# Running log-sum-exp over 4 x 4096 x 4128: two-row tiles moved inside the batches, the engine order put off around them, and loads by rows for two tiles only

## Chip, cores and metric

The kernel runs on one core of a Trainium2 chip. The metric is the device time in microseconds of one execution; less is better. All data are float32, and the program is one launch.

## What is computed

For each of 4 batches and each of 4128 columns, a running log-sum-exp down 4096 rows:

```python
B, S, D = (4, 4096, 4128)
out[:, 0, :] = x[:, 0, :]
for t in range(1, S):
    mx = np.maximum(out[:, t - 1, :], x[:, t, :])
    out[:, t, :] = mx + np.log(np.exp(out[:, t - 1, :] - mx) + np.exp(x[:, t, :] - mx))
```

The input is normally distributed, so the kernel takes exp of it as it is, forms running sums, and takes the log. At the end it looks at the smallest first rows and the largest sums and branches to a slow general routine (`_general`) if they left a safe range; here they don't. The input is 270.5 MB and so is the output.

## The kernel before

**Tiles.** A tile is 128 x r consecutive rows of one batch, all 4128 columns, with r = 2 or 3: partition p holds rows r*p to r*p + r - 1 one behind the other, so a tile is one contiguous stretch of DRAM of r x 2064 KB. The lists `begin`, `usual` and `final` (lines 176 to 178) give r for the tiles of batch 0, of batches 1 and 2, and of batch 3: 12 + 11 + 11 + 12 = 46 tiles, ten with two rows ("short" tiles) and 36 with three, numbered 0 to 45 in the order in which they run. Four slots in SBUF hold four tiles; a tile is loaded, worked on in place, and stored from its slot.

**Work on a tile.** Its columns are cut into three chunks of 1376 (`Chunk`). For each chunk:

- `exp` on ACT (line 113), over all rows of the chunk.
- `sums` on DVE (lines 133 and 135): the sum over the partition's rows, into a buffer z for chunks 0 and 1, into the tile's last row for chunk 2.
- `head` on PE (line 142): a matmul with a triangular matrix, which gives each partition the sum of all rows above it into PSUM. For chunks 0 and 1 the running total of the tiles before comes in with z's last row. For chunk 2 `fold` (line 123) adds it to the first row on DVE, ahead of its `sums`.
- `add` on DVE (lines 157 and 165, or line 150 for chunk 2): the sum from above onto the rows.
- `log` on ACT (lines 173 and 174, or line 169 for chunk 2).

`least` (line 116) and `total` (line 126) run once per batch and chunk and serve the test of the range. There are two PSUM buffers, taken in turn.

**The order of the work is written out by hand.** Each engine has a list, built in the loop over tiles (lines 238 to 253), and runs it strictly in order, waiting for what each step needs. What varies by tile is the "turn": `turns.get(t, usual_turn)` gives two rows of four numbers. The first says how many chunks of tile t+1 have had their `exp` put on ACT's list before the `log` of tile t's chunk 0, chunk 1 and chunk 2, and after it. The second says the same of tile t+1's `sums` on DVE ahead of the `add` of tile t. The usual turn is `(0, 2, 3, 3), (0, 0, 1, 1)`: two `exp` of the next tile before the `log` of chunk 1, the third before that of chunk 2, and one `sums` of the next tile before the `add` of chunk 2. Six turns differ, at tiles 0 to 3, n-3 and n-2 (n = 46).

**Transfers.** All loads and stores are issued by SP, on one queue, in the order of the list `moves` (lines 193 to 202): loads 0 to 3, stores 0 and 1, then load 4, store 2, load 5, store 3 and so on; the last two loads follow each other. SP waits for what each needs (a store for its tile's last `log`, a load for the store that frees its slot) and issues nothing behind it until then. There are eight semaphores for transfers, taken in turn, so a transfer also waits until the one eight before it has landed. A tile's load is one transfer (line 93), but for tiles 0 to 6 (`BY_ROW = 7`) it is one transfer for each of its r rows (line 96).

Of the kernel before, what the change touches and what calls it, by code (L numbers as in the profile page):

```python
# [13 lines left out]
MM = 512  # L14
NC = 3
SLOTS = 4
BY_ROW = 7
PASSED = NC - 1
SMALL = 2.0 ** -63
LARGE = 2.0 ** 62  # L20
# [3 lines left out]
def kernel(  # L24
# [57 lines left out]
    class Step:  # L82
# [6 lines left out]
            return rows.rearrange("(p j) d -> p j d", j=self.r)  # L89

        def load(self):
            if self.n >= BY_ROW:
                nc.sync.dma_start(out=self.xt, in_=self.dram(x))
                return
            for j in range(self.r):
                nc.sync.dma_start(out=self.xt[:, j, :], in_=self.dram(x)[:, j, :])
# [76 lines left out]
            nc.scalar.activation(e, e, ACT.Ln)  # L173
            nc.scalar.activation(self.row[r - 1], self.z, ACT.Ln)  # L174

    begin = [2, 2, 3, 3, 3, 3, 3, 3, 3, 3, 2, 2]
    usual = [2, 3, 3, 3, 3, 3, 3, 3, 3, 3, 3]
    final = [2, 3, 3, 3, 3, 3, 3, 3, 3, 2, 2, 2]
    steps = []
    for b in range(B):  # L180
        row = 0
# [9 lines left out]
    n = len(steps)  # L191
# [3 lines left out]
    for t in range(n):  # L195
# [8 lines left out]
    lists = {"move": moves, "act": [], "vec": [], "pe": []}  # L204
    act, vec, pe = lists["act"], lists["vec"], lists["pe"]
    usual_turn = (0, 2, 3, 3), (0, 0, 1, 1)
    turns = {
# [4 lines left out]
        n - 3: ((0, 0, 3, 3), (0, 0, 0, 0)),  # L212
        n - 2: ((1, 2, 3, 3), (0, 0, 1, 1)),
    }
    given = {"exp": [0] * n, "sums": [0] * n}
# [158 lines left out]
```

## Time and profile before

| | us |
|---|---|
| median of 3 timed runs | 1266.24 (1265.36 to 1266.4) |
| the profiled execution, its own time | 1262.61 |
| its span, first to last instruction | 1260.6 |
| busy: DVE | 1047.2 (83%) |
| busy: ACT | 926.1 (73%) |
| busy: PE matmul | 601.3 (48%) |
| bytes moved over the span | 429 GB/s |

"Busy" is the time in which an engine had an instruction of the program under way. The profile gives the DMA engines' busy share beside it, and the chain of work that ended last, followed back from the end. Times in the views are counted from the first instruction. In the views of the profile, L12 is line 12 of the kernel, and SPq is SP's instruction queue.

### The profile page before, as it was taken

How to read it: one execution, taken by the hardware profiler on the slowest of the kernel's cores; microseconds unless marked ns; L12 is line 12 of the kernel's file. 1: busy time of each engine (PE TensorE's matmuls, PEld its weight loads, DVE VectorE, ACT ScalarE, POOL GpSimd, SP SyncE). 2: the span in 40 equal slices, each digit the busy share in tenths (PEclk: the TensorE clock that was granted, in tenths of full speed). 3: DMA queues.
4: the chain of work that ended last, by engine and by line, in shares of the span. 5: the costliest groups of instructions: out<-in, count | busy, mean ns of one | idle time of the engine just before them, and what ended most of it. 6: DMA issues, size and time to landing. Idle time of an engine off the chain costs nothing.

```text
span 1260.6 us, 3131 instructions
## 1 busy us (share of the span) xinstructions
PE 601.3 (48%) x830; PEld 233.9 (19%) x830; DVE 1047.2 (83%) x547; ACT 926.1 (73%) x369; POOL 3.8 (0%) x15
## 2 busy tenths in 40 slices
PE   3544444464545444445444544455454454445662
PEld 1221111121222111111111211121121121111220
DVE  4999888895899877888978978888897797888984
ACT  5968777776678677777857777777776677777882
POOL 1000000000000000000000000000000000000000
PEclk9866666676677676666765666666675666666676
DMA  9999999999999999999999999999999999999998
GB/s 398 426 441 427 428 435 434 424 434 431 438 434 429 425 443 434 429 428 436 429 442 428 439 432 428 433 442 429 429 435 426 434 412 442 430 429 433 430 423 375
DMA packets 14994, 541.28 MB, mean 429 GB/s; under 512 B 1664, under 2 KB 1664, under 8 KB 1664
## 3 DMA queue, kind: packets, MB, share of 16 engines
q1 hardware_dynamic: 14976, 541.07, 99.7%
q8 instruction: 7, 0.11, 0.0%
q14 instruction: 11, 0.09, 0.0%
HBM read 270.53 MB, written 270.53 MB: 429 GB/s over the span
## 4 chain that ended last, share of the span: by engine, by line
DMA 61%; ACT 22%; DVE 9%; issue 6%; SPq 1%; ACTq 0%; DVEq 0%
DMA x<-in_x_dram 57%; ACT x L113 11%; ACT x L169 5%; ACT x L173 4%; DMA out_dram<-x 4%; DVE x L150 2%; ACT x L174 2%; DVE x L157 2%; DVE z L135 1%; DVE x L133 1%; DVE z L160 1%; DVE x L135 0%; DVE x L123 0%; SPq L99 0%; DVE short L116 0%
## 5 line engine op out<-in xcount | busy, mean ns | idle before, releaser
L113 ACT ACTIVATE x<-x 128x4128 f32<-128x4128 f32 (+1 forms) x138 | 462.3, 3382 | 183.7 <-DMA x<-in_x_dram 183.6
L142 PE MATMUL p<-z,carried 128*128 128x512 f32 (+1 forms) x504 | 375.2, 910 | 456.4 <-DVE z L135 297.0
L173 ACT ACTIVATE x<-x 128x2752 f32<-128x2752 f32 (+1 forms) x92 | 206.0, 2239 | 129.7 <-DVE z L165 117.1
L133 DVE TENSOR_TENSOR x<-x 128x1376 f32<-128x1376 f32 x108 | 171.2, 1585 | 146.8 <-ACT x L113 146.8
L142 PEld LDWEIGHTS p<-z,carried 128*128 128x128 f32 x504 | 145.8, 309 | 687.4 <-DVE z L135 331.6
L142 PE MATMUL p<-x,summed 128*128 128x512 f32 (+1 forms) x276 | 194.3, 867 | 130.9 <-issue 125.1
L157 DVE TENSOR_TENSOR x<-p,x 128x2752 f32<-128x2752 f32 (+1 forms) x92 | 248.2, 2698 | 0.9 <-PE p L142 0.8
L150 DVE SCALAR_TENSOR_TENSOR x<-p,inner,x 128x4128 f32<-128x4128 f32 (+1 forms) x46 | 193.1, 4198 | 0.6 <-PE p L142 0.5
L135 DVE TENSOR_TENSOR z<-x 127x1376 f32<-127x1376 f32 x92 | 146.3, 1590 | 39.5 <-ACT x L113 33.7
L169 ACT ACTIVATE x<-x 128x4128 f32<-128x4128 f32 (+1 forms) x46 | 155.5, 3379 | 2.4 <-DVE x L150 2.4
L165 DVE TENSOR_TENSOR z<-x 128x1376 f32<-128x1376 f32 x84 | 133.8, 1592 | 2.9
L174 ACT ACTIVATE x<-z 128x1376 f32<-128x1376 f32 x92 | 122.7, 1333 | 0.0
L142 PEld LDWEIGHTS p<-x,summed 128*128 128x128 f32 x276 | 75.3, 290 | 248.5 <-issue 245.9
L135 DVE TENSOR_TENSOR x<-x 128x1376 f32<-128x1376 f32 x46 | 73.2, 1590 | 1.2
L123 DVE TENSOR_TENSOR x<-p,x 1x1376 f32<-1x1376 f32 x42 | 66.1, 1573 | 2.8 <-ACT x L113 2.4
L142 PE MATMUL p<-z,below 128*128 128x512 f32 (+1 forms) x48 | 31.9, 827 | 48.4 <-DVE z L135 28.7
L142 PEld LDWEIGHTS p<-z,below 128*128 128x128 f32 x48 | 12.7, 280 | 66.6 <-issue 31.0
L116 DVE TENSOR_REDUCE short<-x 1x1 f32<-1x1376 f32 x12 | 18.7, 1566 | 0.0
L160 DVE CUSTOM_DVE_ANT_0 z<-x 128x1376 f32<-128x1376 f32 x8 | 12.7, 1592 | 0.3
L126 DVE TENSOR_REDUCE probe<-p 1x1 f32<-1x1376 f32 x4 | 6.3, 1568 | 0.0
L308 PE MATMUL good<-ones,low 128*1 128x1 f32 x2 | 0.2, 164 | 5.5 <-DVE low L306 5.5
L74 POOL MEMSET z<- 128x1376 f32 x2 | 2.5, 1258 | 0.0
(21 smaller groups left out, 4.8 us busy)
## 6 DMA issues: line engine op xcount, KB each, us to landing
out_dram<-x SPq DMA_DIRECT2D x36, 6192.0 KB, 26.0
x<-in_x_dram SPq DMA_DIRECT2D x31, 6192.0 KB, 40.1
out_dram<-x SPq DMA_DIRECT2D x10, 4128.0 KB, 22.0
x<-in_x_dram SPq DMA_DIRECT2D x19, 2064.0 KB, 28.2
x<-in_x_dram SPq DMA_DIRECT2D x8, 4128.0 KB, 34.7
```

The costliest lines, as they stand in the source:

```text
L113: nc.scalar.activation(self.e, self.e, ACT.Exp)
L123: nc.vector.tensor_tensor(out=to, in0=pt[0:1], in1=to, op=ALU.add)
L133: nc.vector.tensor_tensor(out=e[1], in0=e[0], in1=e[1], op=ALU.add)
L135: nc.vector.tensor_tensor(out=self.z[0:n], in0=e[r - 2][0:n], in1=e[r - 1][0:n], op=ALU.add,)
L142: nc.tensor.matmul(self.pt[:, a:b], lhsT=w, rhs=self.z[:, a:b], start=True, stop=True,)
L150: nc.vector.scalar_tensor_tensor(out=self.e, in0=base, scalar=inner[:, 0:1], in1=self.e, op0=ALU.mult, op1=ALU.add,)
L157: nc.vector.tensor_tensor(out=e, in0=base, in1=e, op=ALU.add)
L160: nc.vector.tensor_tensor_reduce(out=self.z, in0=ends[0], in1=ends[1], scale=1.0, scalar=0.0, op0=ALU.add, op1=ALU.add, accum_out=probe[:, ...
L165: nc.vector.tensor_tensor(out=self.z, in0=ends[0], in1=ends[1], op=ALU.add)
L169: nc.scalar.activation(self.e, self.e, ACT.Ln)
L173: nc.scalar.activation(e, e, ACT.Ln)
L174: nc.scalar.activation(self.row[r - 1], self.z, ACT.Ln)
```

## The change

Three things are changed.

- The lists of rows per tile: the same number of two-row and three-row tiles in each batch, but the two-row tiles stand inside the batches instead of at their beginnings and ends, except for tiles 0 and 1 and the last two, which stay.
- The turns: a table of 21 entries in place of six. Around the short tiles many are `alone` in their second row (no `sums` of the next tile ahead of this one's `add`), with the `exp` of the next tile put later; some are `(0, 0, 0, 0)`, where nothing of tile t+1 runs on ACT or DVE until the `log` of tile t is on ACT's list. Turns 1 and 3 now put the third `exp` of the next tile ahead of the `log` of chunk 2, and one `sums` of it ahead of the `add` of chunk 2. The turn of n-3 becomes the usual one.
- Loads by rows for tiles 2 and 3 only, in place of tiles 0 to 6.

```diff
-BY_ROW = 7
+BY_ROW = (2, 3)
...
-            if self.n >= BY_ROW:
+            if self.n not in BY_ROW:
                 nc.sync.dma_start(out=self.xt, in_=self.dram(x))
...
-    begin = [2, 2, 3, 3, 3, 3, 3, 3, 3, 3, 2, 2]
-    usual = [2, 3, 3, 3, 3, 3, 3, 3, 3, 3, 3]
-    final = [2, 3, 3, 3, 3, 3, 3, 3, 3, 2, 2, 2]
+    begin = [2, 2, 3, 3, 3, 3, 2, 3, 2, 3, 3, 3]
+    usual = [3, 3, 3, 3, 3, 2, 3, 3, 3, 3, 3]
+    final = [3, 3, 3, 3, 2, 3, 2, 3, 3, 3, 2, 2]
...
     usual_turn = (0, 2, 3, 3), (0, 0, 1, 1)
+    alone = (0, 0, 0, 0)
     turns = {
         0: ((2, 3, 3, 3), (0, 0, 1, 1)),
-        1: ((1, 2, 2, 2), (0, 0, 0, 0)),
-        2: ((3, 3, 3, 3), (0, 0, 0, 0)),
-        3: ((2, 2, 3, 3), (0, 0, 0, 0)),
-        n - 3: ((0, 0, 3, 3), (0, 0, 0, 0)),
+        1: ((1, 2, 3, 3), (0, 0, 1, 1)),
+        2: ((3, 3, 3, 3), alone),
+        3: ((1, 2, 3, 3), (0, 0, 1, 1)),
+        6: ((0, 0, 0, 0), alone),
+        7: ((0, 0, 0, 0), alone),
+        9: ((0, 0, 1, 1), alone),
+        10: ((0, 2, 2, 2), alone),
+        11: ((0, 1, 2, 2), alone),
+        12: ((0, 2, 2, 2), alone),
+        13: ((0, 2, 2, 2), alone),
+        15: ((0, 1, 1, 1), alone),
+        17: ((0, 0, 3, 3), alone),
+        18: ((0, 0, 0, 0), alone),
+        26: ((0, 0, 1, 1), alone),
+        28: ((0, 0, 3, 3), alone),
+        29: ((0, 0, 0, 0), alone),
+        n - 10: ((0, 0, 1, 1), alone),
+        n - 8: ((0, 0, 1, 1), alone),
+        n - 6: ((0, 0, 3, 3), alone),
+        n - 5: ((0, 0, 3, 3), alone),
         n - 2: ((1, 2, 3, 3), (0, 0, 1, 1)),
     }
```

## The prediction

> **What bounds the kernel now.** I read the page first, for how full the DMA engines are.
>
> ```profile
> span 1260.6 us, 3131 instructions
> DMA  9999999999999999999999999999999999999998
> q1 hardware_dynamic: 14976, 541.07, 99.7%
> out_dram<-x SPq DMA_DIRECT2D x36, 6192.0 KB, 26.0
> x<-in_x_dram SPq DMA_DIRECT2D x31, 6192.0 KB, 40.1
> out_dram<-x SPq DMA_DIRECT2D x10, 4128.0 KB, 22.0
> x<-in_x_dram SPq DMA_DIRECT2D x19, 2064.0 KB, 28.2
> x<-in_x_dram SPq DMA_DIRECT2D x8, 4128.0 KB, 34.7
> ```
>
> One queue carries 541 MB, and its packets fill 99.7% of sixteen engines' span. The busy digit is 9 in 39 of the 40 slices. The last five rows are the transfers by kind: the last number of each is the time from issue to landing, so it holds the wait in the queue too. Whether the queue is ever empty is asked of a table of windows (us, busy time of PE, PEld, DVE, ACT and POOL, granted clock, DMA share, GB/s):
>
> ```profile
> 2.00:50.00 48.00, 20.71 (x36) 8.46 (x36) 34.02 (x21) 33.76 (x18) 2.36 (x6) 0.92 1.00 425
> 10.00:48.00 38.00, 20.71 (x36) 8.46 (x36) 32.02 (x20) 31.67 (x16) 0.00 (x0) 0.91 1.01 431
> 350.00:600.00 250.00, 121.70 (x162) 47.04 (x160) 213.98 (x106) 188.25 (x71) 0.00 (x0) 0.66 1.00 433
> 2.00:1246.00 1244.00, 601.34 (x830) 233.89 (x830) 1047.24 (x547) 924.94 (x369) 2.36 (x6) 0.67 1.00 431
> 1246.00:1261.00 15.00, 0.00 (x0) 0.00 (x0) 0.00 (x0) 0.00 (x0) 0.00 (x0) 0.50 0.71 303
> ```
>
> From 2 us to 1246 us the DMA share is 1.00. DVE is busy 1047 of those 1244 us and ACT 925, so neither fills the time. The kernel is a full transfer queue with under 2 us ahead of it and the last store's end behind it. So a change can win time only by moving the same bytes faster, and can lose time only where it lets the queue run dry.
>
> The second question is how close it comes to running dry. The chain of waits lists transfers from issue to landing (start, us, what):
>
> ```profile
> 38.21 24.71 DMA out_dram<-x
> ...
> 377.57 35.17 DMA x<-in_x_dram
> ...
> 548.06 40.14 DMA x<-in_x_dram
> 588.23 3.65 ACT x L113
> ...
> 689.45 35.26 DMA x<-in_x_dram
> ...
> 1003.25 36.19 DMA x<-in_x_dram
> ...
> 1195.51 20.07 DMA x<-in_x_dram
> ```
>
> At 433 GB/s a transfer of 6192 KB (6.34 MB) takes 14.6 us, one of 4128 KB 9.8, one of 2064 KB 4.9. The load issued at 548.06 landed 40.14 us later. It stood right behind a three-row store, so 40.1 - 2 x 14.6 = 10.9 us of work was still ahead of that store when it was issued. I call that the store's cover: what the queue holds when the store joins it, the start-up of the transfer included. The loads at 377.57, 689.45 and 1003.25 also follow three-row stores, and give 6.0, 6.1 and 7.0 us. Those are the thin places, and the share stays at 1.00 there too.
>
> **The cover, worked from the order.** SP issues store t, load t+3, store t+1, load t+4. Behind load t+1 the queue holds store t-1 and load t+2, and then store t. In a usual turn ACT runs two Exp of tile t+1 before the middle Ln of tile t, so store t follows the landing of load t+1 by a fixed lag:
>
> ```profile
> 606.12 0.34 SPq L99 DMA_DIRECT2D out_dram<-x  x1
> ...
> 1195.93 47.23 SPq L99 DMA_DIRECT2D out_dram<-x  x4
> ...
> 1214.82 0.34 SPq L99 DMA_DIRECT2D out_dram<-x  x1
> ...
> DMA to landing us min/median/max: 16.9/26.0/34.3
> L113 ACT ACTIVATE x<-x 128x4128 f32<-128x4128 f32 x108 | 388.8, 3632 | 155.2 <-DMA x<-in_x_dram 155.2
> L113 ACT ACTIVATE x<-x 128x2752 f32<-128x2752 f32 x30 | 73.5, 2485 | 28.5 <-DMA x<-in_x_dram 28.5
> ```
>
> The load landed at 588.2 (the Exp starts at 588.23) and the store was issued at 606.12: lag 17.9 us. The cover is store t-1 plus load t+2 less 17.9: 29.2 - 17.9 = 11.3 where both have three rows (10.9 was read off), and 24.4 - 17.9 = 6.5 where one of them has two (6.0 to 7.0 read off). So the rule holds to half a microsecond. If tile t+1 is the short one, its three Exp take 2485 instead of 3632 ns, and the lag is 14.5. The last store was issued at 1195.93 + 47.23 - 0.34 = 1242.8 and took 16.9 us to land, 9.8 of them its own: cover 7.1.
>
> **The change part by part.**
>
> *Loads by rows for tiles 2 and 3 only.* Nineteen loads of 2064 KB become six. In their place come three more loads of 6192 KB (34) and two more of 4128 KB (10). The bytes are the same, and there are 96 transfers for 104. The window of row loads alone ran at 431 GB/s, the window of whole-tile transfers at 433. Thirteen row loads fewer are 27.5 MB: 63.8 us at 431, 63.5 at 433, so -0.3 us. The rounding of both rows allows -0.1 to -0.5. If the row of 425, which holds the start, were the rate, it would be -1.2. I take -0.4, nearest to the cleaner pair of rows. No Exp waits differently for it, since each Exp reads all the rows of its tile.
>
> In the windows of row loads, ten transfers in 48 us left the share at 1.00, so no time between queued transfers shows. The Trainium skill's page "DMA: Bandwidth & Descriptors", in its section "Anatomy of one DMA — SWDGE (gpsimd) path", gives each DMA of another queue kind a fixed cost of about 2.0 us whatever its size. By that rule eight DMAs fewer would be an estimated 16 us; the trace does not bear it out for a full queue.
>
> *The two-row tiles moved inside the batches.* Both kernels have ten two-row and 36 three-row tiles, the same instructions and the same bytes. So nothing is removed on the path, and only the covers move. Before, the joints of the batches put a thin cover of 6 to 7 us at seven stores (8, 13, 21, 24, 32, 35, 41) and 7.1 at the last. After, by the same rule:
>
> - Store 1. Turn 1 now runs a third Exp of tile 2 ahead of the last Ln of tile 1, and DVE the first sums of tile 2 ahead of the last add.
>
> ```profile
> 50.37 2.48 ACT L169 ACTIVATE x<-x 128x2752 f32<-128x2752 f32 x1
> 38.21 15.01 SPq L99 DMA_DIRECT2D out_dram<-x  x2
> 46.31 3.08 DVE L150 SCALAR_TENSOR_TENSOR x<-p,inner,x 128x2752 f32<-128x2752 f32 x1
> ```
>
>   The Ln started at 50.37 and the store followed at 38.21 + 15.01 - 0.34 = 52.9. One Exp more is 3.6 us on ACT; on DVE the add is put off from 46.3 by two additions of 1.6, and ends inside that Exp. So the store is issued at 56.4. The store ahead of it lands at 38.21 + 24.71 = 62.9: cover 6.5 for 10.0.
> - Store 4. Load 6 is short: 14.6 + 9.8 - 17.9 = 6.5, for 11.3.
> - The last store. Tile n-3 has three rows for two. Its store follows the landing of load n-2 by 14.5 us, 9.8 of which load n-1 takes, so 4.7 after load n-1. From that store to the last one is 28.0 us, as before (1214.8 to 1242.8), so 32.7 in all. The queue holds 14.6 + 14.6 + 9.8 = 39.0: cover 6.3 for 7.1.
> - All other usual turns: 10 us or more, the thinnest with a short store ahead and a short tile next, 24.4 - 14.5 = 9.9.
>
> *The turns put off (no Exp of the next tile until the Ln of this one is done).* These make DVE and ACT wait for each other. Queued behind the waiting Exp are all later Exp, and SP's next store behind them. For a three-row tile alone, from its load's landing: one Exp 3.6, two sums of 3.1 each, the fold 1.6, the first add with its z 4.6, the third sum 3.1, the second add 4.6, the last add 4.4, the Ln 3.6: 31.7, about 33 with the hand-overs, for 29.2 of queue. The deepest is tile 7, after the put-off turns 6 and 7: behind its load stand stores 5 and 6 and loads 8 and 9, 14.6 + 9.8 + 9.8 + 14.6 = 48.8, so its store keeps 16 us. By the same sums the covers after the put-off turns 18 and 29 fall from 21 to 11. So these turns cost nothing while their cover is over zero. Should all cover be gone at a place, each us late costs one us, once, and the queue is full again after it.
>
> The order of the tiles, then, makes covers on the whole deeper (three thin ones for eight). Nothing was lost at the thin ones in this trace, so nothing is won there: 0, with a bound below, under the rivals.
>
> *Sum.* The profiled execution took 1262.6 us, 2.0 over its span; it is 3.6 us below the median of the timed runs, 1266.24 (1265.36 to 1266.4). -0.4 makes it 1262.2, and on the median **1265.8 us**.
>
> **The rivals.**
>
> *The timed runs run dry where the profiled one did not (faster).* What the 3.6 us between the profiled execution and the timed median are, the trace doesn't say. If they were all idle queue at the eight thin places, 0.45 each, and the change leaves three, 2.3 us go, with the 0.4 2.7: 1263.5. For it: a cover of 6 us has to hold the start-up of a transfer and whatever the sixteen engines have drifted apart. Against it: a share of 1.00 in every window.
>
> *Store 1 comes too late (slower).* Turn 1 puts an Exp and two additions ahead of a store whose cover was 10.0, and SP holds load 4 behind it. The cover I find is 6.5. Beyond it the queue stands empty: if turn 1 ran 9.5 us later than my sum, 3.0 would be lost, less 0.4: 1268.8. It would decide from an issue after about 62 us. Against it: each duration in the sum for turn 1 has its row, and one Exp is all that is added on ACT. The same price holds for store 4 and the last store.
>
> *The rate itself moves.* One GB/s on the mean of 431 is 2.9 us. The window of 425 GB/s at the start, and the 431 of the whole for 433 in the middle, show that it does move within a run. This widens the range on both sides and is no forecast.
>
> *A fixed price for each transfer (faster).* A share that counts a transfer's own waiting as busy would hide it; then eight transfers fewer at 2.0 us give 1250.2. The 431 against 433 GB/s rule it out as far as they go: a wait of 2 us at each 4.9 us transfer would have cost over a quarter of the rate.
>
> **How the numbers follow.** A measurement of this kernel can tell about 0.2%, 2.5 us, from no change. The forecast (covers hold, -0.4) has 0.73 and lies within it. The dry timed runs have 0.15, and with a rate that rises, and 0.01 for the fixed price, faster is 0.18. Late stores and a falling rate have 0.09 for slower. The range runs from 1262.3 (the dry runs' 1263.5 with half a GB/s more) to 1268.0 (the forecast with 0.8 GB/s less, or 2 us of empty queue).
>
> **What would show it.** Right: a DMA share of 1.00 from 2 us to the last 15, issue of the second store near 56 us and its load's landing unmoved, DVE and ACT busy sums the same, the loads issued right behind stores 13, 21, 24 and 32 landing 40 us or more after issue instead of about 35. Wrong: a window with a share below 1.00 before 1246 us, or an unchanged share with a rate that differs by over 1 GB/s from 431.

## The result, and the profile after

The changed kernel takes 1260.8 us (median of 6 runs, 1260.48 to 1261.45); the kernel before took 1265.8 us beside it (6 runs, 1264.49 to 1267.01). The ratio is 0.9961, with a 95% interval of 0.9948 to 0.9974: 5 us, 0.39%, faster, and no execution of the one overlaps with the other. The range given was 1262.3 to 1268.0 and the forecast 1265.8, so the prediction was wrong: the gain is larger than its whole range allowed. Faster had a chance of 0.18.

The page of the changed kernel:

```profile
span 1259.1 us, 3098 instructions
DMA  9999999999999999999999999999999999999998
q1 hardware_dynamic: 13824, 541.07, 99.6%
out_dram<-x SPq DMA_DIRECT2D x36, 6192.0 KB, 26.1
x<-in_x_dram SPq DMA_DIRECT2D x34, 6192.0 KB, 40.2
```

Nothing on it says where 5 us went: the queue is as full as before, and DVE and ACT are as busy. The span is only 1.5 us shorter than that of the profiled execution before. The other 3.5 us are mostly a matter of which execution of the kernel before was profiled: at 1262.61 us it was quicker than every timed one of that kernel (1262.65 to 1268.0). The same kernel run again left a profile at 1267.25 us. Windows of both profiles of the kernel before (the first row from the prediction's profile, the next from the second one), then of the changed kernel; columns as before, share and GB/s last:

```profile
600.00:1150.00 550.00, 260.43 (x348) 101.02 (x348) 463.90 (x239) 405.05 (x155) 0.00 (x0) 0.65 1.00 432
```

```profile
600.00:665.00 65.00, 28.58 (x45) 11.25 (x43) 55.41 (x33) 45.10 (x20) 0.00 (x0) 0.71 1.00 424
...
600.00:1150.00 550.00, 257.01 (x348) 99.34 (x347) 461.21 (x237) 404.81 (x155) 0.00 (x0) 0.66 1.00 430
```

```profile
2.00:1240.00 1238.00, 587.96 (x828) 229.02 (x828) 1048.48 (x542) 923.52 (x369) 2.36 (x6) 0.67 1.00 432
...
600.00:1150.00 550.00, 257.14 (x354) 99.75 (x354) 464.83 (x239) 402.81 (x158) 0.00 (x0) 0.65 1.00 433
```

The share is 1.00 in all of them, yet the rate from 600 to 1150 us is 432, 430 and 433: the DMA engines are busy, and some of their packets take longer. The second profile of the kernel before has 424 GB/s from 600 to 665 us, right behind its thin store 21.

A transfer is cut into packets, and the trace holds each packet with its time. A packet of 16512, 33024 or 49536 bytes takes 615, 1222 or 1829 ns nearly always (96 to 97% of them, to 10 ns). What packets took above that, summed and divided by sixteen engines, I call slow time: 6.5 us in the profile the prediction used, 9.8 in the second one, 3.6 in the changed kernel. In the changed kernel 2.3 of these lie in the first 200 us. So the queue moved its bytes more slowly at some places, and those places are to be found. (Against the prediction's profile the changed kernel has 3 us less slow time, and its span is still only 1.5 us shorter. It gives 1.6 us back at its end, where its engines finish further apart: an engine waits 3.9 us on the mean for the last one, against 2.3.)

### The profile page after: what moved, and what is told of

Its sections match the earlier page's. It is cut to its first block, busy times and chain, and to the rows that moved or that the text cites. A ratio compares the mean times of both kernels' runs of the same rounds, so it can differ in the third digit from the quotient of the medians.

```text
span 1259.1 us, 3098 instructions
## 1 busy us (share of the span) xinstructions
PE 588.1 (47%) x830; PEld 229.1 (18%) x830; DVE 1049.8 (83%) x547; ACT 926.5 (74%) x369; POOL 3.8 (0%) x15
## 4 chain that ended last, share of the span: by engine, by line
DMA 56%; ACT 24%; DVE 10%; issue 4%; PE 2%; SPq 0%; ACTq 0%; DVEq 0%
DMA x<-in_x_dram 47%; ACT x L113 14%; DMA out_dram<-x 8%; ACT x L169 5%; ACT x L173 3%; DVE x L157 3%; DVE x L150 2%; PE p L142 2%; ACT x L174 2%; DVE x L123 1%; DVE x L133 1%; DVE z L165 1%; DVE z L135 1%; DVE x L135 1%; SPq L99 0%
## 5 line engine op out<-in xcount | busy, mean ns | idle before, releaser
L142 PE MATMUL p<-z,carried 128*128 128x512 f32 (+1 forms) x504 | 361.0, 880 | 450.8 <-DVE z L135 302.5
L142 PEld LDWEIGHTS p<-z,carried 128*128 128x128 f32 x504 | 140.0, 296 | 671.6 <-DVE z L135 336.1
L142 PE MATMUL p<-z,below 128*128 128x512 f32 (+1 forms) x48 | 35.8, 916 | 60.0 <-DVE z L135 43.1
```

The source lines that it names most:

```text
L142: nc.tensor.matmul(self.pt[:, a:b], lhsT=w, rhs=self.z[:, a:b], start=True, stop=True,)
```

## The experiments

I call a store thin where the prediction's rule gives it a cover of 6 to 7 us. Two explanations stood at the start. By the thin covers theory the time is lost at the thin stores; by the row loads theory it is lost where tiles are loaded by rows.

Every experiment ran beside the kernel before: 1 to 3 beside a median of 1266.53 us, 4 to 6 beside 1266.55, 7 beside 1266.14, with executions from 1262.65 to 1268.0. The changed kernel itself ran beside 1265.8, so differences from its 1260.8 compare across these sets and are good to about half a microsecond. Kernels without thin stores inside the batches scatter over about 1 us.

**1. The kernel before again, and its loads alone.** The first is unchanged. The second:

```diff
-BY_ROW = 7
+BY_ROW = (2, 3)
-            if self.n >= BY_ROW:
+            if self.n not in BY_ROW:
```

> The kernel before, unchanged, for a second profile of it and a look at its scatter. Both theories: ratio 1.000. Thin covers theory (the queue, or some of its sixteen engines, runs short in most executions at the thin stores 8, 13, 21, 24, 32, 35 and 41): executions between 1264 and 1267 us, and a profile near that median shows lost time (a lower share or slow packets) at or after these stores. Row loads theory: the lost time lies in the first 165 us, where the row loads run, in this profile too.

> The kernel before with loads by rows for tiles 2 and 3 only; its tile lists and turns stay. Thin covers theory: -0.4 to -0.6 us, ratio 0.9996, about 1265.3, since the covers of the seven thin stores stay at 6 to 7 us. Row loads theory: nearly all of the 5 us, ratio 0.9965, about 1261.

Measured 1266.33 (ratio 1.0002, 0.9993 to 1.0011) and 1266.06 us (0.9995, 0.9985 to 1.0005). The loads alone make no difference clear of the noise, so they aren't where 5 us went. The packets give their size: three of 16512 bytes take 3 x 615 = 1845 ns where one of 49536 takes 1829, and over the kernel this and the like for two-row tiles make 0.5 us; the prediction had 0.4. Of the slow time of the second profile, 8.1 of 9.8 us lie after the first 165 us, and 7.0 of these within 45 us behind the thin stores.

**2. The order alone.** The changed kernel with `BY_ROW = 7` and its old test.

> The changed kernel with loads by rows for tiles 0 to 6, as before; its tile lists and turns stay. Thin covers theory: -4.5 us, ratio 0.9965, about 1261.3. Row loads theory: about 1265.3, ratio 0.9996.

Measured 1261.42 us (0.9964, 0.9951 to 0.9976). The tile lists and turns bring nearly all of it.

**3. The new tile lists with the usual turns.** The transfers are those of the changed kernel; only what ACT and DVE do ahead differs. Of the 22 entries in the table of turns, 17 go.

```diff
-        6: ((0, 0, 0, 0), alone),
...
-        n - 5: ((0, 0, 3, 3), alone),
```

> The changed kernel (its tile lists and its loads) with the usual turn for tiles 4 to n-3, so with none of the put-off turns there. The transfers and their order are those of the changed kernel; only the covers differ: by the rule stores 9, 15, 18, 26, 29, 36 and 41 come down to 6.5 us. Thin covers theory: most of the gain is gone, 1264 to 1266 us, ratio 0.999 to 1.000. A theory by which the place of the short tiles itself, or the loads, brought the gain: about 1261, ratio 0.996.

Measured 1265.78 us (0.9992, 0.9984 to 1.0001): the gain is gone. The place of the short tiles brings nothing that shows by itself.

**4. The old tile lists with turns put off.**

```diff
+    turns[8] = ((0, 0, 0, 0), (0, 0, 0, 0))
+    turns[9] = ((0, 2, 2, 2), (0, 0, 0, 0))
+    turns[12] = ((0, 0, 0, 0), (0, 0, 0, 0))
+    turns[13] = ((0, 2, 2, 2), (0, 0, 0, 0))
+    turns[14] = ((0, 2, 2, 2), (0, 0, 0, 0))
+    turns[24] = ((0, 0, 1, 1), (0, 0, 0, 0))
+    turns[35] = ((0, 0, 1, 1), (0, 0, 0, 0))
+    turns[41] = ((0, 0, 1, 1), (0, 0, 0, 0))
```

> The kernel before (its tile lists and its loads) with eight turns put off, at tiles 8, 9, 12, 13, 14, 24, 35 and 41. By the rule five of the seven thin stores get covers of 9 us or more; only stores 21 and 32 stay at 6.5. Thin covers theory: the loss goes with the number of thin stores, 5 us for 7, so 5 x 0.7 = 3.6 us less: ratio 0.997, about 1262.8. A theory by which the new places of the short tiles are needed: no change, ratio 1.000.

Measured 1262.72 us (0.9970, 0.9957 to 0.9982). With 2 and 3 this shows where the time goes: it is lost with the thin stores, whichever tiles make them, and comes back when they are given more cover.

**5. Two thin stores, and one dry one, in the changed kernel.** The first takes the entries 26, 28 and 29 out of the table of turns. The second adds one:

```diff
+    turns[26] = ((3, 3, 3, 3), (0, 0, 1, 1))
```

> The changed kernel with the usual turn at tiles 26, 28 and 29, so that by the rule just two stores inside the batches are thin, 26 and 29, at 6.5 us. Thin covers theory: 2 x 0.7 = 1.4 us over the changed kernel, about 1262.2, and slow packets only in the 35 us behind those two stores. If it takes many thin stores to lose anything: 1260.8.

> The changed kernel with all Exp of tile 27 put ahead of the first Ln of tile 26: by the rule the cover of store 26 is -1.3 us, so all engines run dry there, by 2.8 us with the start-up. Idle theory (what is lost at a thin store is the idle time of the engines itself): +2.8 us, about 1263.6, packets at full speed afterwards. Step theory (engines that run dry start again in step and then get in each other's way where the queue turns from stores to loads and back): +2.8 and about 1.3 more, about 1264.9, with slow packets on all engines about 15 and 29 us after the restart.

Measured 1262.42 us (1261.78 to 1262.74; 0.9966, 0.9952 to 0.9979) and 1266.38 us (0.9995, 0.9986 to 1.0004). The first is 1.6 us over the changed kernel, and as much over the kernel of experiment 6, which has no thin store inside the batches either, ran in the same set and stayed within 1260.4 to 1261.43: 0.8 us for each thin store. Windows of the changed kernel, of the one with thin stores 26 and 29, and of the one with store 26 dry:

```profile
750.00:790.00 40.00, 20.03 (x30) 7.83 (x30) 34.86 (x18) 26.60 (x14) 0.00 (x0) 0.70 1.01 436
```

```profile
700.00:750.00 50.00, 22.85 (x30) 8.95 (x30) 40.26 (x21) 37.51 (x15) 0.00 (x0) 0.67 1.00 430
750.00:790.00 40.00, 19.88 (x30) 7.87 (x30) 29.82 (x16) 24.22 (x12) 0.00 (x0) 0.67 1.01 423
```

```profile
745.00:765.00 20.00, 9.46 (x12) 3.66 (x12) 16.35 (x8) 11.88 (x6) 0.00 (x0) 0.55 0.85 368
765.00:795.00 30.00, 15.04 (x24) 6.12 (x24) 26.50 (x15) 26.29 (x14) 0.00 (x0) 0.75 0.97 396
```

The thin store 26 was issued at 752.9 us. The share does not fall, but the rate goes from 436 to 423 GB/s over 40 us. In the trace ten packets are slow at 767 to 771 us and 21 at 782 to 789 us: at the end of that store and at the end of the load behind it. Around the dry store, issued at 758.2 us, the share falls to 0.85 (3.0 us of 20 idle; the sum had 2.8), and 26 and 18 slow packets come at the same two places, at 772 to 777 and 786 to 790 us, where the step theory had put them. The dry store cost 5.6 us, more than both theories said: beside the 3.0 idle its profile has 2.3 us more slow time than the changed kernel's, 1.8 of it in that store and the load behind it. The engines left store 26 within 0.7 us of each other in the dry case, within 4.3 us in the thin one. Both have slow packets, so running in step is not needed for them.

**6. Higher covers at the start.** The changed kernel with `1: ((1, 2, 2, 2), alone)`, `3: ((1, 2, 2, 2), alone)` and `4: ((0, 1, 1, 1), alone)`.

> The changed kernel with three more turns put off, at tiles 1, 3 and 4, so that by the rule the covers of stores 1, 3 and 4 rise from 6.0, 7.7 and 6.5 to over 9 us. Thin covers theory: what is still lost at stores 1 and 4 goes, at most 1.4 us, about 1259.5 to 1260.5; the slow packets of the first 200 us grow fewer. If the stores of the start cost nothing: 1260.8.

Measured 1260.82 us (0.9954, 0.9940 to 0.9967), not to be told from the changed kernel. The slow time of the first 200 us was 2.1 for 2.3 us, so most of it does not come from thin covers. The thin stores 1 and 4 cost nothing that shows. So a thin cover has no price by itself, and something else has to be added. The trace suggests what: each transfer ends with sixteen small packets (4 bytes), one for each engine. The first and last of these are 0.6 us apart in the first transfer of the changed kernel, 3.3 at 140 us, 4.6 at 613 and 6.6 at 1232 us. The spread stays as it is for hundreds of microseconds, so the engines have the same bytes, but they drift apart in steps. I had counted the cover up to the last engine. Counted up to the first one (from the end of the store's issue to the first small packet of the transfer ahead), with the slow time in that store and the next load (to about 0.1 us, by where one draws the edges), by the packets of five profiles, all in us:

```
kernel                 store  issued  cover, last  cover, first  slow time
changed                  4      137       5.7          2.4         0.10
before, first profile    8      255       5.8          2.3         0.14
before, first profile   24      689       5.7          2.1         0.08
before, first profile   13      377       5.7          1.6         0.18
before, first profile   35     1003       5.8          0.8         1.07
before, second profile  13      377       5.7          1.4         0.40
before, second profile  24      692       5.8          0.9         0.97
before, second profile  21      608       5.9          0.2         1.42
before, second profile  32      923       5.7         -0.3         1.41
thin 26 and 29          29      837       5.8          1.2         0.71
thin 26 and 29          26      753       5.7          0.8         1.16
new tiles, usual turns   9      269       5.8          2.3         0.04
new tiles, usual turns  18      524       5.8          1.2         0.83
new tiles, usual turns  26      755       5.7         -0.1         1.37
```

The last column follows the first engine's cover: 0.04 to 0.14 us from 2.1 up, about 1 us at 1, and 1.4 where that engine runs dry. The cover to the last engine is 5.7 to 5.9 in every row and tells nothing. The other thin stores inside the batches, in all twelve profiles, fit this (store 41, behind which two loads follow each other, only if 45 us behind it are counted); between 1.5 and 2.2 us they scatter, from under 0.1 to 0.7.

**7. Two thin stores early, two late.** The changed kernel without the entries 9 to 13 and 15, and without n-10, n-8, n-6 and n-5.

> The changed kernel with the usual turn at tiles 9 to 13 and 15, so that by the rule just stores 9 and 15 inside the batches are thin, at 6.5 us, early in the run (about 270 and 440 us). Theory of one price for each thin store: +1.4 us over the changed kernel, about 1262.2, as with stores 26 and 29. Drift theory (the cover that counts is the one of the DMA engine that has run furthest ahead, and the sixteen drift apart as the run goes on: 3.5 us at 270 us, 4.2 at 440, 5 and more behind 600): little is lost, 0.3 to 0.5 us, about 1261.2, and packets slow down hardly at all behind store 9.

> The changed kernel with the usual turn at tiles 36, 38, 40 and 41, so that by the rule just stores 36 and 41 inside the batches are thin, at 6.5 us, late in the run (about 1040 and 1170 us). Theory of one price for each thin store: +1.4 us, about 1262.2. Drift theory: at least as much as at stores 26 and 29, +1.6 to +2.6 us, 1262.4 to 1263.4, with slow packets on all engines behind both.

Measured 1261.32 us (1260.16 to 1262.72; 0.9964, 0.9950 to 0.9978) and 1262.69 us (0.9973, 0.9964 to 0.9982). The medians fall as the drift theory has them: 0.5 us over the changed kernel for two early ones, 1.9 for two late ones. The 1.9 is clear of the scatter (1261.62 to 1263.03); the 0.5 is not. The profiled execution of the early kernel was its slowest, 1262.72 us: there the engines had drifted 5.7 us apart by 442 us already, not 4.2, the first engine's cover at store 15 was 0.1 us, and the slow time 1.4. The same store 15 in the profile of experiment 3, at 440 us with a drift of 4.2 and 1.5 us left to the first engine, had under 0.4. So what goes with the loss is the drift and not the hour, and the drift differs from run to run. No run changed the drift by itself. The late one shows the loss in its windows, first the changed kernel's and then its own:

```profile
1030.00:1070.00 40.00, 22.73 (x35) 8.83 (x33) 36.59 (x19) 28.62 (x14) 0.00 (x0) 0.71 1.01 439
```

```profile
1030.00:1070.00 40.00, 20.53 (x33) 8.01 (x31) 33.93 (x19) 27.91 (x13) 0.00 (x0) 0.71 0.99 414
```

## Why the prediction was wrong

**What held.** The bound (a full queue) and the covers, step by step. The changed kernel's issues and landings:

```profile
38.27 18.54 SPq L99 DMA_DIRECT2D out_dram<-x  x2
...
137.15 0.33 SPq L99 DMA_DIRECT2D out_dram<-x  x1
```

```profile
1193.23 48.92 SPq L99 DMA_DIRECT2D out_dram<-x  x4
```

```profile
DMA to landing us min/median/max: 16.3/26.0/37.2
```

```profile
605.92 41.08 DMA x<-in_x_dram
```

Store 1 was issued at 38.27 + 18.54 - 0.33 = 56.5 us; the sum for turn 1 had 56.4. It took 16.3 us to land, the shortest of all, 9.8 of them its own: cover 6.5, as the sum had it. The last store went out at 1241.8 and took 16.4 us: cover 6.6, against 6.3. The load behind store 21 landed 41.1 us after its issue, where thin ones had taken 35. The loads by rows were sized rightly: 0.5 us by the packets, and medians that allow it with the old order (0.9995) and the new one (1261.42 to 1260.8), though neither is clear of the noise; the sum had 0.4. So the signs that the prediction named as right came out, as far as the rows show them, and still the time was another. Its sign for a moved rate was too coarse: from 2 us on the rate went from 431 to 432 GB/s, within the 1 GB/s that it allowed.

**The step that failed** is "Nothing was lost at the thin ones in this trace, so nothing is won there: 0". It should have been 4.5 to 5 us, about 0.7 for each of the seven thin stores inside the batches. It was wrong twice. First, the cover was read off the landing of a transfer, which is that of its last engine, while the slow packets follow what the engine furthest ahead still has. At 6 us of the one, the other had 0.8 to 2.3 us. Secondly, something was lost in that very trace, 3.3 us of slow time within 45 us behind its seven thin stores: a DMA share of 1.00 counts slow packets as busy. The table of windows had it in a row that the prediction does not use, 950 to 1050 us in the kernel before:

```profile
950.00:1050.00 100.00, 45.93 (x63) 18.08 (x62) 78.51 (x40) 72.94 (x28) 0.00 (x0) 0.62 1.00 426
```

Seven GB/s under the 433 of the middle is 1.6 us in 100, behind stores 32 and 35; the packets have 1.9 us of slow time there. Even a line that the prediction shows had it: it read a cover of 7.0 us off the load that landed 36.19 us after its issue at 1003.25, where the loads behind the other thin stores gave 6.0 and 6.1. The packets have the cover at 5.8 there as well, and 1.1 us of slow time: the extra microsecond was the loss.

**The rivals.** The first one, that the timed runs lose time at the thin places, was the right one. Its price, 2.3 us for five places fewer and 0.4 for the loads, was too small. It was sized by the 3.6 us between the profiled execution and the median, as if that execution had lost nothing, though it had 2.9 us more slow time than the changed kernel's. Nor did the time go as idle queue, as the rival had it, but as slow packets. Measured are 5.0 us in all, with the loads. A thin store cost 0.7 to 0.8 us on the mean (5.1 us for seven in experiment 2, 3.8 for five in experiment 4), and by the packets single ones cost from under 0.1 to 1.5. It also named the drift of the sixteen engines as what speaks for it, and gave it 0.15 because of the share. Store 1 was not late, and no put-off turn cost anything that shows, as forecast. The fixed price of 2 us for each transfer did not show: experiment 1, with eight transfers fewer, has an interval that ends at 1.9 us, far from 16.

**Not settled.** Why packets are slow on most engines at the two turns of the queue behind a thin store (from the store to the load, and from that load to the next store), where nothing lacks in the queue any more, was not found. A thin cover without such a turn behind it seems to cost little: at the last store of the changed kernel the first engine had run dry 0.7 us before the issue, and the slow time was 0.1 us. What sets the pace of the drift was not tested either. The page of the changed kernel has a lead, two small queues of instruction packets beside q1 (packets, MB, share):

```profile
q8 instruction: 7, 0.11, 0.0%
q14 instruction: 11, 0.09, 0.0%
```

From 200 to 1232 us the sixteen engines' lags behind the first one grow by 20 us in sum. 14 of these fall in the 16 of 74 transfers during which one of these packets ran, and the three steps of about 1 us in the spread (at 613, 866 and 1115 us) each come within 8 us of one. In the first 200 us most of the growth has no such packet beside it.

## What to carry to other kernels

A busy share of 1.00 does not show that a queue loses nothing: compare the rate of the same stretch between runs and between long windows of one, and where it falls by 1 to 2%, compare the times of packets of one size. Where one queue is spread over sixteen engines, the reserve ahead of each transfer has to cover the drift between them too: here 9 us to the last engine was enough (with a drift of 6.5), and 6 was mostly not once the drift passed 4 us. And see where the profiled execution stands among the timed ones before its losses are taken for the kernel's.

## What was not expected of the hardware

- The sixteen DMA engines, given equal bytes by one queue, drifted apart from 0.6 to 6.6 us over 1.2 ms, and harmlessly so while the queue stayed deep enough: the changed kernel at 6.5 us apart, with 2.7 us left to the first engine, lost 0.02 us at store 41.
- Where the queue was short for the first engines (1.2 us left or less), packets of most engines were slow up to 36 us later: 0.7 to 1.4 us in the store and the load behind it, at a share of 0.99 to 1.01.
- A store that found its queue empty started its first packet 0.8 us after its issue (758.23 to 759.07 us in the dry kernel).
